# Feed-forward products in two passes: 512 columns over both halves of the activations, then 256

## The chip, the cores and the metric

The kernel runs on one core of a Trainium2 chip. The metric is the device time of one execution in microseconds (us): the kernel before takes 1524.75 us (median of three runs, 1522.54 to 1529.18). Lower is better.

## What is computed

Three layers over 256 tokens of 1024 features, in float32: two layers of a first block (feed-forward, mixer, feed-forward) and one of a second block (mixer, feed-forward). The change touches the five feed-forward stages alone:

```python
def swiglu(h, w_gate_up, w_down):          # four times, first block
    a, b = jnp.split(h @ w_gate_up, 2, axis=-1)
    return (jax.nn.silu(a) * b) @ w_down
x = x + 0.5 * swiglu(rms_norm(x, g), w_gate_up, w_down)

h2 = rmsnorm(x, norm2_w)                   # once, second block
a, v = jnp.split(h2 @ ffn_w_up, 2, axis=-1)
a = jax.nn.gelu(causal_dwconv(a, ffn_conv_w, ffn_conv_b), approximate=False)
x = x + (a * v) @ ffn_w_down               # 1024 -> 2 * 2816, then 2816 -> 1024
```

## The kernel before

**Products.** A float32 product is made of three: each operand is cut into a high and a low half (`wh`, `wl` of the weights, `ahi`, `alo` of the activations), and `mm3` (lines 192 to 194) adds `wl`·`ahi`, `wh`·`alo` and `wh`·`ahi` in one PSUM bank. Features stand on the partitions: a tile of 128 x 128 weights is the stationary operand, 256 tokens are the moving one. Below, a triple is the three products of one weight tile.

**Weights.** They stream from HBM in units of 128 x 2048 (1 MB, 16 weight tiles), in the order of use. `split` (line 151 is its VectorE half) cuts them, in feed-forward stages half a unit at a time: ScalarE copies 128 x 1024 (`wh<-raw`, line 86, the copy helper), VectorE subtracts (`wl<-raw,wh`). Three units lie raw, four are split (`SPLITS`): while a chunk of two units is in use, the two of the next are split.

**Order.** The program is written out by hand, in one order per engine. `tick()` stands after each step of products; it emits deferred work that is due (`defer(n, f)`: n ticks later), then one split. Each engine works its list strictly in order.

**A feed-forward stage.** `feed_forward` takes eleven chunks of 512 weight columns: four column tiles of 128, of which 0 and 2 are gates and 1 and 3 the ungated halves; each tile has eight k-tiles, so 32 triples a chunk. In `cols` a tick stands after every four triples. `emit` works on pairs: VectorE multiplies the gate by the norm's factor (`sl<-ps,rbc`, line 436), ScalarE takes Silu (line 437), VectorE multiplies by the other half (`hh<-ps,sl`, line 422), ScalarE cuts the high half (`ahi<-hh`), GpSimd subtracts for the low one (`alo<-hh,ahi`, line 421). In the second block the gate goes through a convolution (lines 443 to 450) and Gelu. Then `rows_out` makes the down projection, eight column tiles of 22 triples each; `add_to_x` adds each onto the residual stream `xT` with two VectorE instructions (lines 375, 376), and `Norm.done` cuts it for the next stage. The first stage has its first two chunks in `opening`, the others chunk 0 in `cols` with the norm's mean between.

Of the kernel before, what the change touches and what calls it, by code (L numbers as in the profile page):

```python
# [8 lines left out]
F = mybir.dt.float32  # L9
R = mybir.dt.float32r  # L10
# [4 lines left out]
P = 128  # L15
# [16 lines left out]
# columns of the row parameters  # L32
# [3 lines left out]
def weave(main, fill, ratio=1.0):  # L36
    """emit main's steps with `ratio` steps of fill after each"""
    due = 0.0
    for _ in main:
        due += ratio  # L40
        while due >= 1.0:
            next(fill, None)
            due -= 1.0


def drain(gen, plan={}):
    """emit gen to its end; plan[n] is emitted after its step n"""
    for n, _ in enumerate(gen):
        if n in plan:
            plan[n]()  # L50
# [3 lines left out]
def tile_hybrid_stack(ctx, tc, wts, cst, prm, rows, small, out, x):  # L54
# [4 lines left out]
    up = pool("acts", 35)  # L59
# [28 lines left out]
    class Acts:  # L88
        """activations split for the products, features on the partitions, one k-tile of 128 at a time"""

        def __init__(self):
            self.t = {}

        def get(self, k):
            if k // 2 not in self.t:
# [8 lines left out]
    # the weights' stream: (source, elements per partition) in the order of use  # L104
# [32 lines left out]
    def split(m):  # L137
        """m quarters of the next unit"""
# [18 lines left out]
    # work of the other engines that is emitted some steps of dense products later  # L157
# [12 lines left out]
    def tick():  # L170
        """what the other engines do beside a step of dense products"""
# [8 lines left out]
    def units(n, more=False):  # L180
        """the next n units; all before them are done with, but for `more` of the last ones"""
# [14 lines left out]
    def col_part(ps, acts, nk, unit_, k0, c0, pitch=512):  # L196
        """four k-tiles of a tile of 128 weight columns (on partitions) times all tokens"""
# [6 lines left out]
    def cols(acts, nk, emit, norm=None):  # L204
        """a chunk of 512 weight columns; emit(i, ps, ps) gets column tiles 2i and 2i + 1"""
# [26 lines left out]

    def opening(norm, emit0, emit1):
        """the first two chunks, k-tile by k-tile as they arrive; the mean of squares comes last"""
# [24 lines left out]
    def toks(acts, emit, n=512, norm=None):  # L259
        """all tokens (on partitions) times a chunk of n weight columns; emit(t, ps)"""  # L260
# [64 lines left out]
    class Norm:  # L325
        """the residual stream's tiles as they are done: split for the products, and their mean square"""

        def __init__(self, gcol):
            self.gcol = gcol
            self.acts = Acts()  # L330

        def done(self, j):
            """tile j of the residual stream is final"""
# [35 lines left out]
    def add_to_x(norm, scale, rb):  # L369
        def emit(j, ps):  # L370
            if rb is None:
                nc.vector.tensor_tensor(xT[:, j], ps, xT[:, j], OP.add)
            else:
                d = wt("dx")
                nc.vector.tensor_tensor(d, ps, rb, OP.mult)  # L375
                nc.vector.scalar_tensor_tensor(xT[:, j], d, scale, xT[:, j], op0=OP.mult, op1=OP.add)  # L376
            if norm is None:
                nc.sync.dma_start(out[:, j], xT[:, j])
            else:
                norm.done(j)  # L380
        return emit

# [23 lines left out]
    def feed_forward(norm, gate, nxt, scale, first=False, beside=None):  # L406
        """up and gate projections with features on the partitions; the norm's factor of the
        ungated half is applied to the sums of the down projection, which it commutes with"""
        hT = Acts()
        pace[0] = 2  # L410

        def emit(j):
            def f(i, pg, pu, both=None):
                k = 2 * j + i
                a, n = gate(k, pg)
                v = wt("hh")

                def last():
                    dh, dl = hT.get(k)
                    copy(dh, v)  # L420
                    nc.gpsimd.tensor_tensor(dl, v, dh.bitcast(F), OP.subtract)  # L421
                defer(n, lambda: nc.vector.tensor_tensor(v, pu, a, OP.mult))  # L422
                defer(n + 1, last)
            return f
# [9 lines left out]
    def silu_gate(f, ps):  # L434
        a = wt("sl")
        nc.vector.tensor_tensor(a, ps, RS["bc"], OP.mult)  # L436
        nc.scalar.activation(a, a, AF.Silu)  # L437
        return a, 1

    def conv_gate(f, ps):  # L440
        w = lambda k: pr[:, P_FCW + 3 * f + k:P_FCW + 3 * f + k + 1]
        z, a = wt("cz"), wt("sl")
        nc.vector.tensor_tensor(z, ps, RS["bc"], OP.mult)
        nc.scalar.activation(a, z, AF.Identity, scale=w(2), bias=pr[:, P_FCB + f:P_FCB + f + 1])
# [4 lines left out]
        defer(1, rest)  # L449
        defer(2, lambda: nc.scalar.activation(a, a, AF.Gelu))  # L450
        return a, 3

# [1 line left out]
    def rope_tables(col, rcol, n, name):  # L454
        """the gains folded into the rotation's tables, for n gains of 64"""
# [24 lines left out]
    def head_roots(sq, n, d, name):  # L480
        """(mean of squares + eps) ** -0.5 of sq [P, n, d] -> [P, n]"""
# [16 lines left out]
    def to_heads(src, dst, t):  # L498
        """[P, 512] -> dst [2] x [P, 2, S], features on the partitions"""
# [70 lines left out]
    def soft_rows(ps, mask, nscale, mn, rsum, p):  # L570
        """s = (ps + mask) * nscale, mn = min of s; p = exp(mn - s), rsum = its row sums"""
# [9 lines left out]
    def staged(n, *stages):  # L581
        """software pipeline: in round r, stage (lag, f) of item r - lag"""
# [7 lines left out]
    def mixer1(l, norm, nxt, tables):  # L590
# [51 lines left out]
        def window_means(k, t):  # L642
            """mean of the last 2 ** (k + 1) tokens less the token itself"""
# [106 lines left out]
    def mixer2(norm, nxt, tables):  # L750
# [13 lines left out]
        # mLSTM queries (k-tiles 0, 1) and keys (2, 3): causal convolution along the tokens  # L764
# [22 lines left out]
        # kw | vw | small gates  # L787
# [9 lines left out]
        # log forget gates, both token tiles at once: log_sigmoid(f) = min(f, 0) - log1p(exp(-|f|)),  # L797
        # log1p(e) = 2 atanh(e / (2 + e))
# [45 lines left out]
        # mLSTM heads  # L844
# [93 lines left out]
        # attention queries  # L938
# [49 lines left out]
        def windows(i):  # L988
            """the blocks to compress: [(half, d), l, (group, n)], half h holding position l + 16 h"""
# [54 lines left out]
        # attention over the selected (0) and window (1) branches  # L1044
# [45 lines left out]
        # the compressed branch  # L1090
# [112 lines left out]
    norm = Norm(P_L)  # L1203
# [7 lines left out]
    for l in range(2):  # L1211
# [6 lines left out]
        norm, nxt = nxt, Norm(pb + 16)  # L1218
        mixer1(l, norm, nxt, tabs)
        norm, nxt = nxt, Norm(P_L + P_LN if l == 0 else P_N1)  # L1220
# [4 lines left out]
    nxt = Norm(P_N2)  # L1225
# [35 lines left out]
def _rows_of(w, kt):  # L1261
    """[K, N] -> units of kt k-tiles, each [128, kt, N] in memory order"""
# [4 lines left out]
def _tiles_of(w):  # L1267
    """[K, N] -> units of 16 tiles [128, 128], column tile by column tile"""
# [94 lines left out]
```

## Time and profile before

| | |
|---|---|
| time, median of 3 runs | 1524.75 us (1522.54 to 1529.18) |
| profiled execution, first to last instruction (its span; its own time is not given) | 1519.0 us |
| granted TensorE clock, mean | 0.998 |
| busy: TensorE, VectorE, ScalarE, GpSimd | 99%, 65%, 50%, 21% |
| DMA | 261.86 MB, mean 172 GB/s |

In the rows PE is TensorE's matmuls, PEld its weight loads, DVE VectorE, ACT ScalarE, POOL GpSimd. A matmul's duration overlaps that of its neighbours, so what one costs is the distance between two starts. A row of the timeline gives start and length in us; "x2" is two instructions merged; brackets hold the idle time before and who ended it.

### The profile page before, as it was taken

The page shows a single profiled execution, that of the slowest core. Times are in us where ns is not written, and L with a number is a line of the kernel's source. Part 1 is how long each engine was busy: PE and PEld are TensorE (multiplying, and loading weights), DVE is VectorE, ACT ScalarE, POOL GpSimd, SP SyncE. Part 2 cuts the span into 40 slices and gives each one's busy share as a digit, 9 for nine tenths or more (in the row PEclk, how much of TensorE's full clock was granted, in tenths as well). Part 3 has the DMA queues.
Part 4 walks back from the last instruction along what each step waited for, and adds up shares of the span by engine and source line. Part 5 has one row for each costly group of instructions (what it writes and reads, how often), then busy time and mean ns, then how long its engine had stood idle before and what let it go on. Part 6 is the DMA issues. An engine that isn't in the chain of part 4 may idle for free. (4 is left out here: it accounts for less than half of the span.)

```text
span 1519.0 us, 28268 instructions
## 1 busy us (share of the span) xinstructions
PE 1500.6 (99%) x11806; PEld 1455.6 (96%) x11806; DVE 981.6 (65%) x1503; ACT 752.2 (50%) x1275; POOL 321.8 (21%) x393
## 2 busy tenths in 40 slices
PE   7999999999999999999999999999999999999998
PEld 7999988999999999999989999999987889999998
DVE  6666568577655655656585686566676667877662
ACT  5544345455444444444455654444457736555541
POOL 3311144013111121111360042111233011421200
PEclk9999999999999999999999999999999999999999
DMA  7555535444555544555443455556443423555551
GB/s 283 187 185 201 198 122 191 140 159 175 183 181 192 205 157 172 190 194 194 175 167 112 167 170 191 190 172 214 162 167 111 167 84 138 184 181 192 194 213 39
DMA packets 38720, 261.86 MB, mean 172 GB/s; under 512 B 4288, under 2 KB 5824, under 8 KB 7744
## 3 DMA queue, kind: packets, MB, share of 16 engines
q1 hardware_dynamic: 38016, 259.08, 48.2%
q8 instruction: 92, 1.51, 0.4%
q10 hardware_dynamic: 576, 0.98, 0.2%
q14 instruction: 36, 0.29, 0.1%
HBM read 258.99 MB, written 1.05 MB: 171 GB/s over the span
## 5 line engine op out<-in xcount | busy, mean ns | idle before, releaser
L192 PE MATMUL ps<-ahi,wl 128*128 128x256 f32 x3472 | 994.7, 286 | 8.0 <-DVE wl L151 7.1
L193 PE MATMUL ps<-alo,wh 128*128 128x256 f32 x3472 | 983.6, 283 | 0.0
L194 PE MATMUL ps<-ahi,wh 128*128 128x256 f32 x3472 | 983.4, 283 | 0.0
L151 DVE TENSOR_TENSOR wl<-raw,wh 128x1024 fp32r<-128x1024 f32 (+2 forms) x605 | 639.6, 1095 | 116.7 <-ACT wh L86 116.1
L192 PEld LDWEIGHTS ps<-ahi,wl 128*128 128x128 f32 x3472 | 667.1, 192 | 19.4 <-DVE wl L151 9.9
L193 PEld LDWEIGHTS ps<-alo,wh 128*128 128x128 f32 x3472 | 667.5, 192 | 0.3
L194 PEld LDWEIGHTS ps<-ahi,wh 128*128 128x128 f32 x3472 | 667.2, 192 | 0.0
L86 ACT ACTIVATE wh<-raw 128x1024 fp32r<-128x1024 f32 (+2 forms) x605 | 506.7, 881 | 69.0 <-PE ps L194 33.1
L421 POOL TENSOR_TENSOR alo<-hh,ahi 128x256 fp32r<-128x256 f32 x110 | 98.3, 894 | 493.0 <-ACT ahi L86 492.8
L437 ACT ACTIVATE sl<-sl 128x256 f32<-128x256 f32 x88 | 36.6, 417 | 218.1 <-DVE sl L436 218.0
L86 ACT ACTIVATE ahi<-xT,pr 128x256 fp32r<-128x256 f32 x64 | 32.2, 507 | 154.9 <-DVE xT L376 119.5
L422 DVE TENSOR_TENSOR hh<-ps,sl 128x256 f32<-128x256 f32 x108 | 45.6, 423 | 64.2 <-ACT sl L437 54.0
L436 DVE TENSOR_TENSOR sl<-ps,rbc 128x256 f32<-128x256 f32 x86 | 36.4, 424 | 78.0 <-PE ps L194 75.7
L342 POOL TENSOR_TENSOR sq<-xT 128x256 f32<-128x256 f32 x56 | 36.8, 657 | 202.6 <-DVE xT L376 181.1
L375 DVE TENSOR_TENSOR dx<-ps,rbc 128x256 f32<-128x256 f32 x40 | 17.0, 425 | 88.2 <-PE ps L194 88.2
L192 PE MATMUL ps<-wh,alo 128*128 128x512 f32 (+1 forms) x176 | 69.9, 397 | 0.0
L193 PE MATMUL ps<-wl,ahi 128*128 128x512 f32 (+1 forms) x176 | 67.8, 385 | 1.3 <-DVE wl L151 1.3
L86 ACT ACTIVATE ahi<-hh 128x256 fp32r<-128x256 f32 x110 | 44.9, 410 | 46.8 <-DVE hh L422 46.8
L194 PE MATMUL ps<-wh,ahi 128*128 128x512 f32 (+1 forms) x176 | 67.8, 385 | 0.0
L346 DVE SCALAR_TENSOR_TENSOR alo<-xT,pr,ahi 128x256 fp32r<-128x256 f32 x64 | 36.2, 569 | 30.0 <-ACT ahi L86 29.9
L560 POOL TENSOR_TENSOR alo<-g,ahi 128x512 fp32r<-128x512 f32 x9 | 13.3, 1483 | 182.0 <-ACT ahi L86 182.0
L343 POOL TENSOR_TENSOR sums<-sums,sq 128x256 f32<-128x256 f32 x56 | 49.2, 878 | 4.4
(251 smaller groups left out, 963.5 us busy)
## 6 DMA issues: line engine op xcount, KB each, us to landing
raw<-wts SPq DMA_DIRECT2D x241, 1024.0 KB, 4.8
raw<-wts SPq DMA_DIRECT2D x2, 576.0 KB, 4.3
raw<-wts SPq DMA_DIRECT2D x4, 256.0 KB, 5.7
raw<-wts SPq DMA_DIRECT2D x2, 512.0 KB, 8.2
out_dram<-xT SPq DMA_DIRECT2D x8, 128.0 KB, 1.9
cs<-cst SPq DMA_DIRECT2D x1, 565.0 KB, 7.2
xT<-x SPq DMA_DIRECT2D x1, 512.0 KB, 7.2
pw<-pool_w ACTq DMA_DIRECT2D x2, 256.0 KB, 3.4
```

Source lines behind the costliest of these rows:

```text
L86: nc.scalar.activation(dst, src, AF.Copy, **kw)
L151: nc.vector.tensor_tensor(lo[:, c], raw[:, c], hi[:, c].bitcast(F), OP.subtract)
L192: nc.tensor.matmul(ps, ll, rh, start=start, stop=False)
L193: nc.tensor.matmul(ps, lh, rl, start=False, stop=False)
L194: nc.tensor.matmul(ps, lh, rh, start=False, stop=stop)
L342: nc.gpsimd.tensor_tensor(sq, xT[:, j], xT[:, j], OP.mult)
L343: nc.gpsimd.tensor_tensor(self.sums, self.sums, sq, OP.add)
L346: nc.vector.scalar_tensor_tensor(dl, xT[:, j], gain, dh.bitcast(F), op0=OP.mult, op1=OP.subtract)
L421: nc.gpsimd.tensor_tensor(dl, v, dh.bitcast(F), OP.subtract)
L422: defer(n, lambda: nc.vector.tensor_tensor(v, pu, a, OP.mult))
L436: nc.vector.tensor_tensor(a, ps, RS["bc"], OP.mult)
L437: nc.scalar.activation(a, a, AF.Silu)
```

## The change

In the feed-forward stages the two halves of an activation tile now lie side by side in one tile (`ahl`, 128 x 512: high, then low). For each column tile `passes` makes eight matmuls of 512 columns (`wh` against both halves), a tick, then eight of 256 (`wl` against the high halves) into the bank's first half. A bank so holds `wh`·hi + `wl`·hi in its first 256 columns and `wh`·lo in its second, and the two have to be added:

- up projection (`wide_cols`, `halves`): ScalarE copies the second half out of PSUM (`wb<-ps`), VectorE adds it to the first (`sl<-ps,wb` or `hh<-ps,wb`), GpSimd multiplies the gate by the norm's factor (`sl<-sl,rbc`) and later the two halves of the pair (`hh<-hh,sl`), both VectorE's before; ScalarE's cut and GpSimd's subtraction stay.
- down projection (`wide_rows`, `add_halves`): ScalarE copies the second half, scaled; GpSimd multiplies it by the norm's factor and adds it onto `xT`; VectorE does the first half as before, one tick later. Each tile is worked in groups of 8, 8 and 6 k-tiles.
- left as before: chunk 0 (the first two chunks in the first stage), the last column tile of each down projection, and both mixers, which keep `mm3`. `acts`, the buffers of activations, goes from 35 to 33; three buffers `wb` of 128 x 256 are new.

TensorE has 2,338 triples of two matmuls in place of three: 1,568 in up projections, 770 in down projections.

```diff
-    up = pool("acts", 35)
+    up = pool("acts", 33)
...
+    def passes(ps, tiles, acts, nk):
+        for k, wh, _ in tiles:
+            nc.tensor.matmul(ps, wh, acts.both(k), start=k == 0, stop=False)
+        tick()
+        yield
+        for k, _, wl in tiles:
+            nc.tensor.matmul(ps[:, 0], wl, acts.both(k)[:, 0], start=False, stop=k == nk - 1)
+
+    def wide_cols(acts, emit):
+        us = units(2)
+        for i in range(4):
+            ps = mm_bank()
+            tiles = [(k, *(u[:, k % 4 * 512 + i * P:k % 4 * 512 + (i + 1) * P] for u in us[k // 4])) for k in range(KT)]
+            yield from passes(ps, tiles, acts, KT)
+            emit(i, ps)
+            tick()
+            yield
...
+    def second_half(ps, **kw):
+        t = sp.tile([P, S], F, tag="wb", name="wb", bufs=3)
+        copy(t, ps[:, 1], **kw)
+        return t
+
+    def add_halves(norm, scale, rb):
+        def emit(j, ps):
+            t, d = second_half(ps, scale=scale), wt("dx")
+            nc.gpsimd.tensor_tensor(t, t, rb, OP.mult)
+            nc.gpsimd.tensor_tensor(xT[:, j], xT[:, j], t, OP.add)
+            nc.vector.tensor_tensor(d, ps[:, 0], rb, OP.mult)
+            defer(1, lambda: onto_x(j, d, norm, scale))
+        return emit
...
+        def halves(j):
+            gated = []
+            def f(i, ps):
+                k = 2 * j + i // 2
+                t = second_half(ps)
+                def add():
+                    z = wt("hh" if i % 2 else "sl")
+                    nc.vector.tensor_tensor(z, ps[:, 0], t, OP.add)
+                    if i % 2 == 0:
+                        nc.gpsimd.tensor_tensor(z, z, rb(), OP.mult)
+                        gated.append(gate(k, z, 1))
+                        return
+                    a, n = gated.pop()
+                    n = max(n - 2, 1)
+                    defer(n, lambda: nc.gpsimd.tensor_tensor(z, z, a, OP.mult))
+                    defer(n + 1, lambda: cut(k, z))
+                defer(1, add)
+            return f
...
-        for j in range(2 if first else 0, 11):
-            drain(cols(norm.acts, KT, emit(j), None if j else norm))
+        if not first:
+            drain(cols(norm.acts, KT, emit(0), norm))
+        for j in range(2 if first else 1, 11):
+            drain(wide_cols(norm.acts, halves(j)))
         flush()
-        drain(rows_out(hT, FT, add_to_x(nxt, scale, RS["bc"])))
+        drain(wide_rows(hT, FT, add_halves(nxt, scale, rb()), add_to_x(nxt, scale, rb())))
```

What this does to the lists of the engines is seen at two places of the first up projection. On ScalarE one chunk stood so (`sl` is Silu, `ahi` the cut of the product):

```order
L86 ACTIVATE wh_740<-raw_536 128x1024 x2
L86 ACTIVATE wh_769<-raw_627 128x1024
L437 ACTIVATE sl_787<-sl_787 128x256
L86 ACTIVATE wh_769<-raw_627 128x1024
L86 ACTIVATE ahi_807<-hh_790 128x256
L437 ACTIVATE sl_850<-sl_850 128x256
L86 ACTIVATE ahi_807<-hh_853 128x256
```

and one chunk stands so in the changed kernel (`wb` is the copy of a bank's second half):

```order
L552 ACTIVATE sl_825<-sl_825 128x256
L86 ACTIVATE wh_840<-raw_732 128x1024
L86 ACTIVATE wb_854<-ps_830 128x256
L86 ACTIVATE wh_840<-raw_732 128x1024
L86 ACTIVATE wb_881<-ps_860 128x256
L86 ACTIVATE ahl_883<-hh_856 128x256
L552 ACTIVATE sl_886<-sl_886 128x256
L86 ACTIVATE wb_907<-ps_889 128x256
L86 ACTIVATE wh_921<-raw_759 128x1024
L86 ACTIVATE wb_932<-ps_911 128x256
L86 ACTIVATE ahl_934<-hh_909 128x256
L86 ACTIVATE wh_921<-raw_759 128x1024
```

Four copies are new, and the weight splits stand singly between a Silu, copies and cuts. On VectorE one chunk and the start of the next stood so:

```order
L436 TENSOR_TENSOR sl_787<-ps_725,rbc_393 128x256
L422 TENSOR_TENSOR hh_790<-ps_725,sl_787 128x256
L151 TENSOR_TENSOR wl_770<-raw_627,wh_769 128x1024 x2
L436 TENSOR_TENSOR sl_850<-ps_794,rbc_393 128x256
L422 TENSOR_TENSOR hh_853<-ps_794,sl_850 128x256
L151 TENSOR_TENSOR wl_871<-raw_666,wh_870 128x1024 x2
```

and stand so now (`sl<-ps,wb` is the addition of a gate's halves, `hh<-ps,wb` that of the other column tile):

```order
L160 TENSOR_TENSOR wl_1146<-raw_983,wh_1145 128x1024 x2
L523 TENSOR_TENSOR hh_1192<-ps_1166,wb_1190 128x256
L160 TENSOR_TENSOR wl_1177<-raw_1068,wh_1176 128x1024 x2
L523 TENSOR_TENSOR sl_1222<-ps_1196,wb_1217 128x256
L523 TENSOR_TENSOR hh_1245<-ps_1225,wb_1243 128x256
L523 TENSOR_TENSOR sl_1273<-ps_1247,wb_1268 128x256
```

Each addition of a tile now stands alone behind its own copy, and a pair's second addition follows two subtractions of weights. GpSimd's list, which had the subtraction `alo<-hh,ahi` alone, is for each pair: `sl<-sl,rbc`, `hh<-hh,sl`, `ahl<-hh,ahl` (lines 525, 530 and 511 of the changed kernel). No DMA is added, and SyncE's list is the same.

## Rows read from the trace of the kernel before

**Rows 1.** The page, part 1: span; busy time, share of it and instructions by engine.

```profile
span 1519.0 us, 28268 instructions
...
PE 1500.6 (99%) x11806; PEld 1455.6 (96%) x11806; DVE 981.6 (65%) x1503; ACT 752.2 (50%) x1275; POOL 321.8 (21%) x393
```

**Rows 2.** The table of stretches: a feed-forward stage, busy us and (instructions) by engine.

```profile
40.00:198.00 158.00, 158.00 (x1319) 158.00 (x1319) 98.25 (x117) 74.69 (x105) 31.80 (x47) 1.00 0.53 187
```

**Rows 3.** Who waited for whom on TensorE: us in total, times, longest us.

```profile
PE ps L192 <- DVE wl L151: 7.1, 7, 5.8
```

**Rows 4.** Timeline of TensorE, up projection: start, us; first and last of 28.

```profile
599.74 0.28 PE L194 MATMUL ps<-ahi,wh 128*128 128x256 f32 x1
...
602.98 0.28 PE L194 MATMUL ps<-ahi,wh 128*128 128x256 f32 x1
```

**Rows 5.** Timeline of TensorE, mixer projection with 512 columns: first and last of 20.

```profile
203.61 0.39 PE L194 MATMUL ps<-wh,ahi 128*128 128x512 f32 x1
...
207.93 0.39 PE L192 MATMUL ps<-wh,alo 128*128 128x512 f32 x1
```

**Rows 6.** Groups of VectorE, shapes apart: busy us, mean ns; idle before, releaser.

```profile
L422 DVE TENSOR_TENSOR hh<-ps,sl 128x256 f32<-128x256 f32 x108 | 45.6, 423 | 64.2 <-ACT sl L437 54.0 <-ACT sl L450 8.8 <-PE ps L194 1.3
...
L447 DVE SCALAR_TENSOR_TENSOR sl<-cz,pr,sl 128x255 f32<-128x255 f32 x22 | 10.7, 487 | 14.2 <-ACT sl L444 14.1
```

**Rows 7.** Groups of ScalarE, shapes apart: a copy out of PSUM of 256 columns.

```profile
L86 ACT ACTIVATE rbc<-rb 128x256 f32<-128x256 f32 x8 | 3.1, 382 | 24.0 <-PE rb L364 24.0
```

**Rows 8.** Line 421, GpSimd: duration ns least/median/most, first and last start.

```profile
L421 POOL TENSOR_TENSOR alo<-hh,ahi x110: 735/745/1664, 39.8 to 1455.4; 128x256 fp32r<-128x256 f32 x110
```

**Rows 9.** Timeline of VectorE at three places where GpSimd works beside it.

```profile
66.14 0.42 DVE L422 TENSOR_TENSOR hh<-ps,sl 128x256 f32<-128x256 f32 x1 [0.61 <-ACT sl L437]
66.49 2.89 DVE L151 TENSOR_TENSOR wl<-raw,wh 128x1024 fp32r<-128x1024 f32 x2
...
223.79 2.13 DVE L151 TENSOR_TENSOR wl<-raw,wh 128x512 fp32r<-128x512 f32 x2
...
1341.50 2.36 DVE L151 TENSOR_TENSOR wl<-raw,wh 128x1024 fp32r<-128x1024 f32 x2 [0.53 <-ACT wh L86]
```

**Rows 10.** Timeline of GpSimd at the same three places.

```profile
67.38 0.92 POOL L421 TENSOR_TENSOR alo<-hh,ahi 128x256 fp32r<-128x256 f32 x1 [5.29 <-ACT ahi L86]
...
224.16 1.22 POOL L477 TENSOR_TENSOR sq<-qk 128x512 f32<-128x512 f32 x1 [1.08 <-ACT qk L86]
225.34 1.18 POOL L471 TENSOR_TENSOR rb<-qk,tks 128x256 f32<-128x256 f32 x1
...
1342.80 1.66 POOL L421 TENSOR_TENSOR alo<-hh,ahi 128x256 fp32r<-128x256 f32 x1 [3.07 <-ACT ahi L86]
```

**Rows 11.** Timeline of ScalarE in an up projection.

```profile
65.62 0.42 ACT L437 ACTIVATE sl<-sl 128x256 f32<-128x256 f32 x1 [1.52 <-DVE sl L436]
65.95 1.04 ACT L86 ACTIVATE wh<-raw 128x1024 fp32r<-128x1024 f32 x1
...
72.68 2.94 ACT L86 ACTIVATE wh<-raw 128x1024 fp32r<-128x1024 f32 x3
```

**Rows 12.** Timeline of TensorE around two waits of the second mixer.

```profile
1126.76 0.50 PE L193 MATMUL ps<-wl,ahi 128*128 128x512 f32 x1 [1.33 <-DVE wl L151]
1127.10 0.40 PE L194 MATMUL ps<-wh,ahi 128*128 128x512 f32 x1
...
1151.19 0.92 PE L1055 MATMUL at<-KT,qT 64*128 64x128 f32 x4 [2.86 <-DVE mn L572]
...
1152.63 0.63 PE L193 MATMUL ps<-wl,ahi 128*128 128x512 f32 x1
1153.06 0.63 PE L194 MATMUL ps<-wh,ahi 128*128 128x512 f32 x1
```

More of the change, by code (lines that the diff above doesn't have):

```diff
@@ L88, in tile_hybrid_stack, with __init__, both @@
     class Acts:
-        def __init__(self):
-            self.t = {}
+        def __init__(self, wide=False):
+            self.t, self.wide = {}, wide
+        def both(self, k):
+            if k not in self.t:
+                self.t[k] = ut([P, 2, S], "ahl", R)
+            return self.t[k]
         def get(self, k):
+            if self.wide:
+                t = self.both(k)
+                return t[:, 0], t[:, 1]
             if k // 2 not in self.t:
@@ L231, in cols, with wide_rows, tile @@
                     yield
+    def passes(ps, tiles, acts, nk):
[14 more added lines that the diff above has]
+            yield
+    def wide_rows(acts, nk, emit, narrow):
+        u0, us = n_used[0], {}
+        def tile(n):
+            return tuple(u[:, n % 16 * P:(n % 16 + 1) * P] for u in us[n // 16])
+        for j in range(KT):
+            ps = mm_bank()
+            for k0 in range(0, nk, 8):
+                ks = range(k0, min(k0 + 8, nk))
+                first, final = j * nk + ks[0], j * nk + ks[-1]
+                n_held[0] = u0 + first // 16
+                for m in range(first // 16, final // 16 + 1):
+                    if m not in us:
+                        us[m] = units(1, True)[0]
+                tiles = [(k, *tile(j * nk + k)) for k in ks]
+                if j < KT - 1:
+                    yield from passes(ps, tiles, acts, nk)
+                    if ks[-1] == nk - 1:
+                        emit(j, ps)
+                else:
+                    for n, (k, wh, wl) in enumerate(tiles):
+                        mm3(ps[:, 0], wh, wl, *acts.get(k), k == 0, k == nk - 1)
+                        if n == 3:
+                            tick()
+                            yield
+                    if ks[-1] == nk - 1:
+                        narrow(j, ps[:, 0])
+                tick()
+                yield
     def opening(norm, emit0, emit1):
@@ L325, in tile_hybrid_stack, with __init__ @@
     class Norm:
-        def __init__(self, gcol):
+        def __init__(self, gcol, wide=False):
             self.gcol = gcol
-            self.acts = Acts()
+            self.acts = Acts(wide)
         def done(self, j):
@@ L375, in emit, with onto_x @@
                 nc.vector.tensor_tensor(d, ps, rb, OP.mult)
[L376 to L380, printed above, removed]
+                onto_x(j, d, norm, scale)
+                return
+            norm.done(j)
+        return emit
+    def onto_x(j, d, norm, scale):
+        nc.vector.scalar_tensor_tensor(xT[:, j], d, scale, xT[:, j], op0=OP.mult, op1=OP.add)
+        if norm is None:
+            nc.sync.dma_start(out[:, j], xT[:, j])
+        else:
+            norm.done(j)
+    def second_half(ps, **kw):
[9 more added lines that the diff above has]
+            defer(1, lambda: onto_x(j, d, norm, scale))
         return emit
@@ L406, in feed_forward @@
     def feed_forward(norm, gate, nxt, scale, first=False, beside=None):
-        hT = Acts()
+        hT = Acts(True)
         pace[0] = 2
+        rb = lambda: RS["bc"]
         def emit(j):
@@ L448, in rest @@
             nc.vector.scalar_tensor_tensor(a[:, 2:], z[:, :S - 2], w(0), a[:, 2:], op0=OP.mult, op1=OP.add)
-        defer(1, rest)
-        defer(2, lambda: nc.scalar.activation(a, a, AF.Gelu))
-        return a, 3
+        defer(1 + later, rest)
+        defer(2 + later, lambda: nc.scalar.activation(a, a, AF.Gelu))
+        return a, 3 + later
     def rope_tables(col, rcol, n, name):
@@ L1200, in mixer2 @@
         drain(rows_out(mT, KT, add_to_x(nxt, 1.0, None)))
-    norm = Norm(P_L)
+    norm = Norm(P_L, True)
     for j in range(KT):
```

42 lines of the change are left out of this document (24 added, 18 removed).

## The prediction

> **What bounds the kernel now.** Read first the page's busy times: VectorE is busy for 982 of 1519 us, ScalarE for 752, GpSimd for 322 [rows 1]. TensorE is the bound: in the first feed-forward stage it is busy for all of 158.00 us at a granted clock of 1.00 [rows 2], and in the whole span its largest wait on one producer is 7.1 us in seven pieces, all but 1.3 of it one piece of 5.8 [rows 3]. So a feed-forward stage lasts as long as its matmuls. What one costs is the distance of starts, not its 0.28 us: 28 matmuls of 256 columns start 0.120 us apart (602.98 - 599.74, over 27) [rows 4]; 20 of 512 columns start 0.227 us apart (207.93 - 203.61, over 19) [rows 5]. The difference, 0.107 us, is 256 columns at 2.4 GHz; so each matmul has a fixed 0.0133 us beside its columns.
>
> **What is saved.** A triple costs 3 x 0.120 = 0.360 us; now 0.227 + 0.120 = 0.3467. All its columns are still there; one fixed part is gone. Over 2,338 triples that is 31.2 us: 20.9 in up projections, 10.3 in down projections. A chunk of 32 triples goes from 11.52 to 11.09 us. DMA then has to bring its two units (2 MB) in 11.09 us, 189 GB/s; it does 187 in that stage now [rows 2]. I cost that at nothing.
>
> The Trainium skill (TensorE: Matmul & The Clock Gate, Back-to-back issue gap) gives an isolated matmul a fixed part of about 2.5 ns; by that the saving would be an estimated 2,338 x 2.5 ns = 6 us. The rows show 13.3 ns here, and I go by them.
>
> **What is added, by sums.** Per chunk ScalarE gets four PSUM copies of 0.38 us [rows 7], and GpSimd six instructions in place of two, each 0.74 us when alone [rows 8]; VectorE has as many as before (four of 0.42, [rows 9]). ScalarE then has four splits that hold it 0.95 each ((2.94 - 1.04)/2) and eight small ones at 0.33 (65.62 to 65.95) [rows 11], 6.4 of 11.09 us. VectorE has four subtractions of weights and four additions, 4 x 1.14 + 4 x 0.34 = 5.9; GpSimd 4.4. By sums all fit. In the old stage they also fitted, with GpSimd at 31.8 of 158 us [rows 2].
>
> **What is added, by the chain.** Each list is worked in order, and the lists now hand to each other at every tile. Two things make this long.
>
> First, VectorE's subtraction of weights and a GpSimd instruction don't run together. At 1341.50 two subtractions end at 1343.86 (1.22 us each, starts 1.14 apart) and the GpSimd one issued at 1342.80 ends 0.60 after them, having taken 1.66 instead of 0.74 [rows 9, 10]. At 67.38 GpSimd got in between two subtractions: it ended at 68.30, and the second subtraction 1.08 later, so that the pair took 2.89 instead of 2.36. They take turns in order of arrival: at 224.16 VectorE came second and still went ahead of GpSimd's next instruction, which was queued already and took 1.18.
>
> Second, the additions (one operand in PSUM) are not held up, but each waits for a copy on ScalarE, and that stands behind a Silu that waits for GpSimd.
>
> Once the chain is behind TensorE, one turn of a chunk is, from Silu to Silu: ScalarE Silu 0.33, copy 0.33, split 0.95, copy 0.38; handover 0.10 (66.14 less the Silu's end at 66.04, [rows 9, 11]); VectorE add 0.34, subtraction 1.22; GpSimd's subtraction 0.60 after it; VectorE's second 1.08; GpSimd's multiplication by the norm's factor 0.60; handover at most 0.10: 6.0. Then Silu 0.33, split 0.95, copy 0.38, handover 0.10, add 0.34, subtraction 1.22, GpSimd's product 0.60, subtraction 1.08, GpSimd's subtraction 0.60, its multiplication 0.74, handover at most 0.10: 6.4. In all 12.4 us; with handovers from GpSimd near nothing, 12.2. I take 12.35 against TensorE's 11.09: **each chunk the weights come 1.26 us later.**
>
> How much lag is free: the chunk's last low part is ready 11.0 us after its Silu (all above but the last 1.4). TensorE asks for it in the second pass of the next chunk's first tile, 11.09 + 8 x 0.227 + 6 x 0.120 = 13.6 us after the chunk's start: 2.6 us. In the first wide chunk the first addition can't start before TensorE has done the tile, at 2.8; from there the chain has 10.3 us left, less about 1.2 since GpSimd's subtraction of the pair before comes early enough to take no turn: it ends at about 11.9, 0.6 to 0.8 late. By the start of the ninth of ten wide chunks the lag is 0.6 + 7 x 1.26 = 9.4, of which 2.6 is free: TensorE waits 6.8 us in an up projection. The down projection asks for the last product about 6.7 us after its start, and the lagging chain (then some 5 us behind, with 3.4 us still to do for it) has it at 8.4: 1.7. Each wait also costs the matmul behind it: after a wait of 1.33 us the next start came 0.34 later, not 0.23 [rows 12]; six of these are 0.6. Sum 9.1 us a stage: three stages 27.3; the first with nine wide chunks 7.8; the last, where the convolution's two instructions of 0.49 [rows 6] stand in the chain beside a longer tail, 10.5. In three stages twelve small GpSimd instructions for rotation tables stand in its list; 1 us each. Together 48.6 us.
>
> **Costed at nothing.** In a down projection GpSimd's two new instructions lengthen the way from a tile to its split by about 2 us out of 7.6; two units split ahead (11 us) cover it; without that cover it is 2 us a tile, 70 us. The last column tile is as before, so the hand-over to the next stage is too. The smaller buffer pool adds waits in the mixers; bounds 0 (the buffers are long free) and 3 us (the largest wait there now is 2.86, [rows 12]); I take 0, as most are on instructions off TensorE's path. The clock: after 2.86 us idle, matmuls of 512 columns started 0.43 apart (1152.63 to 1153.06), 1.2 GHz, after 1.33 us they did not fall [rows 12]; the waits here are of 1.3, so nothing, but it stands close.
>
> **Sum.** -31.2 + 48.6 = +17.4 on a span of 1519.0: 1536. The median of the runs, 1524.75, lies 5.75 above the span, which holds what lies around it; the time is then 1542, and I say 1541.
>
> **Rivals.**
>
> - *The chain keeps pace (faster).* All turns on one point: whether GpSimd's subtraction for the pair before comes before or after the chunk's first subtraction of weights. In the lagging chain I find it 0.17 us after. Coming before, it costs no turn, Silu starts 1.1 us earlier, the turn of a chunk is 11.2 us, and lag stays within the free 2.6 us. Then only the saving is left, 1493.5, and with a few waits up to 1500. For it: the margin is less than two handovers. Against it: once behind, nothing brings the chain back until the down projection.
> - *Half way.* A turn of 11.7 us gives 0.6 a chunk: 0.6 + 7 x 0.6 - 2.6 = 2.2 of waits, with 2 for the end and the rest some 5 a stage, 25 in all: 1519, no change.
> - *Whole turns (slower still).* If whoever loses waits for the whole 0.74 us and then needs its whole 1.22, the chain has 0.14 more at each of four GpSimd places and 0.28 in all more at the two subtractions behind them: 13.2 us, 2.1 a chunk, 15 us a stage: 1570. The Trainium skill (SBUF — State Buffer, Who interferes with whom) states it so: whoever issues first has the shared pair for the whole instruction, and the other fully blocks. The trace agrees that one blocks (1.66 for 0.74), but the handover came earlier than that [rows 9, 10].
> - *The change does not save what it says:* were the fixed part not per matmul, the waits alone would remain, 1573. Rows 4 and 5 speak against it.
>
> **How the numbers follow.** My forecast has 0.47, of which 0.04 falls inside half a per cent (about 7.6 us, what a measurement of this kernel can tell from no change); keeping pace 0.33; half way 0.13; whole turns and no saving 0.07 together. So faster 0.33, same 0.17, slower 0.50. The forecast's own range is 1527 to 1560 (a turn 0.3 us shorter or longer moves five stages by some 17 us). Leaving out keeping pace would leave out 3 in 10, so the range starts at its middle: 1495 to 1562.
>
> **What would show it.** Right: in up projections TensorE waits on VectorE's `wl`, about 1.3 us once a chunk from the fourth or fifth wide chunk on, chunks 12.3 us apart there and 11.1 at the stage's start; matmuls 0.227 and 0.120 apart; GpSimd's instructions between two subtractions of weights longer than 0.74; down projections without waits after their first tile, 7.63 us a tile. Wrong: chunks at 11.1 us throughout, or GpSimd's subtraction ahead of the chunk's first `wl`; a wait on copies or PSUM banks in place of `wl`; a granted clock below 1.00 in a feed-forward stage.

## The result, and the profile after

The changed kernel takes 1544.58 us (median of four runs, 1539.78 to 1548.28); the kernel before, run beside it, 1526.64 (1522.54 to 1529.18). The ratio is 1.0134, with a 95% interval of [1.0104, 1.0164]: 1.3% slower. The forecast was 1541. The span grew by 20.2 us, from 1519.0 [rows 1] to 1539.2; the forecast had 17.4. The profiled execution itself took 1541.0.

The page of the changed kernel, part 1:

```profile
span 1539.2 us, 24143 instructions
...
PE 1486.2 (97%) x9468; PEld 1333.1 (87%) x9468; DVE 1008.2 (66%) x1503; ACT 818.3 (53%) x1506; POOL 665.7 (43%) x659
```

Against [rows 1], TensorE has 2,338 matmuls fewer and falls from 99% to 97%; VectorE has the same 1503 instructions; ScalarE has 231 more and GpSimd 266 more, and GpSimd's busy time doubles. Only TensorE comes near the whole span, so by shares alone no other engine would be in its way. Who waited for whom on TensorE (us in total, times, longest us) says more:

```profile
PE ps L251 <- DVE wl L160: 26.1, 34, 1.0
PE ps L201 <- DVE wl L160: 8.7, 9, 7.1
PE ps L247 <- POOL ahl L511: 6.8, 5, 2.1
...
PE ps L247 <- ACT wh L86: 0.5, 1, 0.5
```

The second row is nearly all the opening, which is in [rows 3] too; its one long wait is 1.3 us longer in this execution (7.1 in place of 5.8). The other three are new: 34 waits of the 256-column pass (line 251) for a low part of weights, one wait at the start of each of the five down projections, for the last activations, and a single short one for a high half of weights. On the timeline of TensorE the waits stand like this in the second feed-forward stage, and at the start of the last down projection (start, length, in brackets the idle time and who ended it):

```profile
381.92 2.00 PE L247 MATMUL ps<-ahl,wh 128*128 128x512 f32 x8
...
426.61 2.00 PE L247 MATMUL ps<-ahl,wh 128*128 128x512 f32 x8
428.45 0.87 PE L251 MATMUL ps<-ahl,wl 128*128 128x256 f32 x6
429.77 0.50 PE L251 MATMUL ps<-ahl,wl 128*128 128x256 f32 x2 [0.45 <-DVE wl L160]
...
466.31 0.51 PE L251 MATMUL ps<-ahl,wl 128*128 128x256 f32 x2 [0.75 <-DVE wl L160]
466.65 2.01 PE L247 MATMUL ps<-ahl,wh 128*128 128x512 f32 x8
...
478.49 0.50 PE L251 MATMUL ps<-ahl,wl 128*128 128x256 f32 x2 [0.74 <-DVE wl L160]
478.83 2.00 PE L247 MATMUL ps<-ahl,wh 128*128 128x512 f32 x8
...
507.47 0.51 PE L247 MATMUL ps<-ahl,wh 128*128 128x512 f32 x1 [1.17 <-POOL ahl L511]
...
531.59 2.00 PE L247 MATMUL ps<-ahl,wh 128*128 128x512 f32 x8
...
539.27 2.00 PE L247 MATMUL ps<-ahl,wh 128*128 128x512 f32 x8
...
1478.49 0.50 PE L247 MATMUL ps<-ahl,wh 128*128 128x512 f32 x1 [2.14 <-POOL ahl L511]
...
1479.55 3.29 PE L247 MATMUL ps<-ahl,wh 128*128 128x512 f32 x8
```

The first wide chunk starts at 381.92, the fifth at 426.61: 11.17 us each, no wait. From the fifth to the tenth there is one wait a chunk, always before the last two of eight matmuls of the first tile's low pass, where the last half of the chunk's second unit is asked for. These six waits stand 12.18 us apart (478.49 - 466.31). So a chunk that needs 11.17 us of TensorE takes 12.18.

The groups of GpSimd's and ScalarE's instructions (busy us, mean ns | idle before, releaser):

```profile
L511 POOL TENSOR_TENSOR ahl<-hh,ahl 128x256 fp32r<-128x256 f32 x110 | 138.2, 1257 | 67.7 <-ACT ahl L86 67.7
L530 POOL TENSOR_TENSOR hh<-hh,sl 128x256 f32<-128x256 f32 x78 | 93.4, 1197 | 139.1 <-DVE hh L523 135.1
...
L525 POOL TENSOR_TENSOR sl<-sl,rbc 128x256 f32<-128x256 f32 x98 | 119.4, 1219 | 29.8 <-DVE sl L523 29.8
L552 ACT ACTIVATE sl<-sl 128x256 f32<-128x256 f32 x88 | 36.7, 418 | 169.6 <-POOL sl L525 168.2
```

Each kind of GpSimd's three instructions per pair takes 1.2 us on the mean, where one alone takes 0.74 [rows 8]. And ScalarE has sat for 168.2 us in front of its 88 Silus, waiting for GpSimd's multiplication; behind each stand a copy or a weight split that needed nothing of it. That number alone proves nothing. In the kernel before, ScalarE sat even longer in front of the same 88 Silus, waiting for VectorE, and TensorE hardly waited [rows 3]:

```profile
L437 ACT ACTIVATE sl<-sl 128x256 f32<-128x256 f32 x88 | 36.6, 417 | 218.1 <-DVE sl L436 218.0
```

Whether the wait matters is for the experiments.

### The profile page after: what moved, and what is told of

The parts are those of the page before. It is cut to its first block, busy times and chain, and to the rows that moved or that the text cites. A ratio compares the mean times of both kernels' runs of the same rounds, so it can differ in the third digit from the quotient of the medians.

```text
span 1539.2 us, 24143 instructions
## 1 busy us (share of the span) xinstructions
PE 1486.2 (97%) x9468; PEld 1333.1 (87%) x9468; DVE 1008.2 (66%) x1503; ACT 818.3 (53%) x1506; POOL 665.7 (43%) x659
## 5 line engine op out<-in xcount | busy, mean ns | idle before, releaser
L247 PE MATMUL ps<-ahl,wh 128*128 128x512 f32 x2338 | 590.0, 393 | 8.0 <-POOL ahl L511 6.8
L247 PEld LDWEIGHTS ps<-ahl,wh 128*128 128x128 f32 x2338 | 420.2, 189 | 85.4 <-POOL ahl L511 9.0
L251 PEld LDWEIGHTS ps<-ahl,wl 128*128 128x128 f32 x2338 | 322.5, 190 | 56.5 <-DVE wl L160 33.0
L251 PE MATMUL ps<-ahl,wl 128*128 128x256 f32 x2338 | 336.5, 284 | 26.1 <-DVE wl L160 26.1
L201 PE MATMUL ps<-ahi,wl 128*128 128x256 f32 x864 | 253.1, 293 | 0.4 <-DVE wl L160 0.4
L202 PE MATMUL ps<-alo,wh 128*128 128x256 f32 x864 | 244.0, 282 | 0.0
L203 PE MATMUL ps<-ahi,wh 128*128 128x256 f32 x864 | 244.0, 282 | 0.0
L201 PEld LDWEIGHTS ps<-ahi,wl 128*128 128x128 f32 x864 | 165.0, 191 | 10.5 <-issue 7.6
L202 PEld LDWEIGHTS ps<-alo,wh 128*128 128x128 f32 x864 | 165.2, 191 | 0.2
L203 PEld LDWEIGHTS ps<-ahi,wh 128*128 128x128 f32 x864 | 165.0, 191 | 0.0
L525 POOL TENSOR_TENSOR sl<-sl,rbc 128x256 f32<-128x256 f32 x98 | 119.4, 1219 | 29.8 <-DVE sl L523 29.8
L552 ACT ACTIVATE sl<-sl 128x256 f32<-128x256 f32 x88 | 36.7, 418 | 169.6 <-POOL sl L525 168.2
L201 PE MATMUL ps<-ahl,wl 128*128 128x256 f32 x270 | 79.3, 294 | 8.4 <-DVE wl L160 8.3
```

What stands on the lines that cost most here:

```text
L201: nc.tensor.matmul(ps, ll, rh, start=start, stop=False)
L202: nc.tensor.matmul(ps, lh, rl, start=False, stop=False)
L203: nc.tensor.matmul(ps, lh, rh, start=False, stop=stop)
L247: nc.tensor.matmul(ps, wh, acts.both(k), start=k == 0, stop=False)
L251: nc.tensor.matmul(ps[:, 0], wl, acts.both(k)[:, 0], start=False, stop=k == nk - 1)
L525: nc.gpsimd.tensor_tensor(z, z, rb(), OP.mult)
```

## The experiments

The theory is the prediction's: in an up projection the lists of ScalarE, VectorE and GpSimd form a chain. It goes round once per chunk in 12.2 us, through ScalarE's waiting Silu and through the turns that VectorE and GpSimd take; whoever makes the chain shorter takes the waits away. There are two rivals. One is the load: VectorE and GpSimd hold each other up, and there is too much work of both, in whatever order (below, the load theory). The other is the units' way from memory. All kernels are the changed one with the edit shown. For each stage, time is counted from its matmul that spreads the norm's factor (`rb<-dg,ones`) to the next one of the kind, and in the last stage to TensorE's end.

**The Silu one step later in the lists, and the same kernel a second time.** The instructions are the same, only their order differs. In the last stage it is the whole gate, the convolution and Gelu, that comes a step later.

```diff
-                        gated.append(gate(k, z, 1))
+                        gated.append(gate(k, z, 2))
```

> One number is changed: the gate's Silu stands one tick later in ScalarE's list, behind the next tile's copy and split instead of ahead of them, so that these no longer wait for GpSimd. Nothing is added or removed. If the chain through all three lists sets the pace (12.2 us a chunk against TensorE's 11.1), cutting it here leaves some 9.8 us a chunk: TensorE's waits on wl in the up projections (34 of them, 26 us) go, those at the start of the down projections (6.8 us) shrink, and the time is 1505 to 1512 us, 2 to 2.5% below the changed kernel and 1% below the kernel before. If VectorE and GpSimd together have too much work that needs their shared reading, or if the weights come too late from memory, the same work is still there: waits and time stay, 1540 to 1548.

> The same kernel as silu_late, on the same chip as both_late for the comparison: 1501 to 1507 us, no waits on wl in the up projections; the span differs from the first time's only by how long the half clock lasts in the second mixer (13.6 us of half clock there).

Measured: 1503.45 us, ratio to the kernel before 0.9863 [0.9837, 0.9889]; the second time 1501.46, 0.9866 [0.9848, 0.9884]. It beats both kernels, and the first time lies below its range of 1505 to 1512. TensorE's waits, the group of Silus, a chunk on ScalarE's timeline and TensorE's passes, all of the first of the two:

```profile
PE ps L201 <- DVE wl L160: 8.1, 6, 7.0
PE at L1170 <- DVE mn L687: 2.9, 1, 2.9
PE ps L247 <- POOL ahl L511: 2.4, 1, 2.4
```

```profile
L552 ACT ACTIVATE sl<-sl 128x256 f32<-128x256 f32 x88 | 36.6, 417 | 11.7 <-POOL sl L525 9.2 <-DVE sl L501 1.4
```

```profile
106.69 2.00 ACT L86 ACTIVATE wh<-raw 128x1024 fp32r<-128x1024 f32 x2
108.89 0.38 ACT L86 ACTIVATE wb<-ps 128x256 f32<-128x256 f32 x1 [0.21 <-PE ps L251]
109.31 0.42 ACT L552 ACTIVATE sl<-sl 128x256 f32<-128x256 f32 x1
109.64 1.05 ACT L86 ACTIVATE wh<-raw 128x1024 fp32r<-128x1024 f32 x1
```

```profile
425.81 2.00 PE L247 MATMUL ps<-ahl,wh 128*128 128x512 f32 x8
427.65 1.12 PE L251 MATMUL ps<-ahl,wl 128*128 128x256 f32 x8
428.60 2.00 PE L247 MATMUL ps<-ahl,wh 128*128 128x512 f32 x8
```

All 34 waits on `wl` are gone, and ScalarE's wait for GpSimd is 9.2 us in place of 168.2: two splits and a copy are now done while GpSimd multiplies. GpSimd's multiplications by the norm's factor are as long as they were (1218 ns on the mean, 1219 in the changed kernel), so the two engines still hold each other up, and TensorE no longer waits for it. Work, operands and loads from memory are the same, so neither the load by itself nor the units' way was the cause. A tile of eight k-tiles takes 2.79 us here (428.60 - 425.81), a chunk 11.17.

**The cut one step later.** This takes GpSimd's subtraction out from between the addition and the multiplication.

```diff
-                    defer(n + 1, lambda: cut(k, z))
+                    defer(n + 2, lambda: cut(k, z))
```

> The cut of the pair before (ScalarE's copy, GpSimd's subtraction) is put one tick later, so that GpSimd's multiplication of the gate comes ahead of that subtraction. If it is this subtraction's turn between VectorE's first two subtractions of weights that makes the chain too long, one turn of each (0.60 + 1.08 us) leaves the way to the Silu, a chunk needs 10.5 us, and TensorE's waits on wl go: 1507 to 1515 us, with the waits at the start of the down projection left (the last product is cut later). If load or memory is the cause: 1540 to 1548 as before.

Measured: 1507.16 us, 0.991 [0.9877, 0.9942]. Waits on `wl` fell from 26.1 us in 34 to 5.6 in 9, all in the first and the last stage; the three stages between take 185.9, 186.8 and 185.9 us, to 0.1 us what they take with the Silu moved. The waits at the start of the down projections, expected to stay, are gone but for 1.7 us in the last. So the prediction's turning point, whether GpSimd's subtraction stands ahead of its multiplication in the lagging chain, is one of the links; ScalarE's order is another, and either is enough in these stages.

**Both later.**

> The chain theory: with the Silu one step later the up projections of the four Silu stages have no waits on wl left, so putting the cut one step later as well has nothing to take away there; the one wait left is 2.4 us at the start of the last down projection, and a later cut can only lengthen it. Stages in the middle 185.5 to 187, time 1500 to 1508, the same as with the Silu alone to within 0.3%. If some other resource (the copies, the pool of buffers, the weights' loads) still held the stages back, two steps of more room would show: under 1497.

Measured: 1501.93 us, 0.9846 [0.9814, 0.9878]: by the medians the same as the Silu alone (1501.46, 0.9866 on the same chip). In the profile, though, the wait of 2.4 us at the last down projection, which I thought could only grow, is gone too, and the last stage takes 177.0 us in place of 181.2. The span did not show it, since the second block's mixer, where nothing differs, took 236.9 us in this execution, at a mean granted clock of 0.95, and 228.0 in the other, at 0.99. Of the executions with a mean clock of 0.999 the one here took 1493.41 us and the one with the Silu alone 1499.91, so the 4 us are there. No new wait comes to light under the old ones.

**The multiplication on VectorE.**

```diff
-                        nc.gpsimd.tensor_tensor(z, z, rb(), OP.mult)
+                        nc.vector.tensor_tensor(z, z, rb(), OP.mult)
```

> The multiplication of the gate by the norm's factor goes back from GpSimd to VectorE (98 instructions of some 0.43 us there, 98 of 0.74 here fewer). By the chain, Silu then follows two VectorE instructions and waits for no turn: about 9.7 us a chunk, no waits on wl, 1503 to 1512 us. By load, VectorE has 0.85 us a chunk more and the shared reading is asked for about as much as before: the waits shrink by a third at most, 1530 to 1545.

Measured: 1507.48 us, 0.9894 [0.9868, 0.992]. VectorE, the busier of the two engines, has 98 instructions more, and the kernel is faster than both; 5.6 us of waits on `wl` are left, all in the last stage. The chain has a handover less, but this run alone does not part the theories: GpSimd's busy time falls too, from 665.7 to 518.9 us, while VectorE's grows from 1008.2 to 1039.9. By the load theory the time was to stay at 1530 or more.

**One GpSimd instruction more, ahead of the gate's multiplication or behind it.** It multiplies the norm's factor by itself into a tile that nobody reads; the two kernels differ in one line's place. The lines that allocate the tile are the same in both and not shown.

Ahead:

```diff
+                        nc.gpsimd.tensor_tensor(junk[0], rb(), rb(), OP.mult)
                         nc.gpsimd.tensor_tensor(z, z, rb(), OP.mult)
```

Behind:

```diff
                         nc.gpsimd.tensor_tensor(z, z, rb(), OP.mult)
+                        nc.gpsimd.tensor_tensor(junk[0], rb(), rb(), OP.mult)
```

> GpSimd gets one idle multiplication more per pair (0.74 us, into a buffer that nobody reads), ahead of the gate's multiplication in its list. By the chain it lies on the way to the Silu in both pairs of a chunk: a chunk's turn grows by 1.4 us to 13.6, some nine chunks in five stages, and the time is 1590 to 1610 us. By load alone (GpSimd goes from 4.4 to 5.9 of 11.1 us a chunk) this run and the one with the same instruction put behind would be alike.

> The same idle GpSimd multiplication per pair as in the run before, but behind the gate's multiplication in GpSimd's list, where GpSimd waits for VectorE's next addition anyway (from 5.9 to 8.2 us of a chunk's turn). By the chain it costs nothing: 1540 to 1550 us, as the changed kernel. By load it costs what it cost in the other place: 1585 to 1595.

Measured, in two executions each: ahead 1590.35 us, 1.0432 [1.038, 1.0483]; behind 1550.8 us, 1.0181 [1.0131, 1.0231]. Two successive waits of the second stage, TensorE's timeline, ahead and then behind:

```profile
443.43 0.50 PE L251 MATMUL ps<-ahl,wl 128*128 128x256 f32 x2 [0.94 <-DVE wl L160]
...
456.75 0.50 PE L251 MATMUL ps<-ahl,wl 128*128 128x256 f32 x2 [0.94 <-DVE wl L160]
```

```profile
453.01 0.51 PE L251 MATMUL ps<-ahl,wl 128*128 128x256 f32 x2 [0.74 <-DVE wl L160]
465.18 0.50 PE L251 MATMUL ps<-ahl,wl 128*128 128x256 f32 x2 [0.74 <-DVE wl L160]
...
1395.62 0.50 PE L251 MATMUL ps<-ahl,wl 128*128 128x256 f32 x2 [1.17 <-DVE wl L160]
1408.60 0.51 PE L251 MATMUL ps<-ahl,wl 128*128 128x256 f32 x2 [1.17 <-DVE wl L160]
```

Ahead, a chunk is 13.32 us long (13.6 expected); behind, 12.17, as in the changed kernel. The load is the same 98 instructions. In the four Silu stages the one behind is free to 0.2 us (187.4, 193.1, 193.9, 193.2 against 187.2, 193.1, 194.0, 193.2), the one ahead costs 10 to 12 us in each. The load theory expected the two to be alike. My bound for gp_after, 1550, was passed by a little: in the last stage, with the convolution gate, it is on the chain (12.98 us a chunk, last two rows, against 12.37; the stage is 6.3 us longer), while the one ahead adds 0.2 us there. Which link of that gate is behind this I did not follow.

**Up projections alone, down projections alone.**

Up alone:

```diff
-            drain(wide_rows(hT, FT, add_halves(nxt, scale, rb()), add_to_x(nxt, scale, rb())))
+            drain(rows_out(hT, FT, add_to_x(nxt, scale, rb())))
```

Down alone:

```diff
-            drain(wide_cols(norm.acts, halves(j)))
+            drain(cols(norm.acts, KT, emit(j)))
```

> The up projections in two passes, the down projections as in the kernel before: 770 triples give back 0.0101 us each (0.3597 before, 0.3496 measured after), 7.8 us, and the last product is asked for some 0.8 us later in five stages. The waits on wl in the up projections stay as they are, since the chain there is the same. 1543 to 1553 us. If the down projection's new GpSimd work were part of the loss, the time would fall below the changed kernel's 1544.

> The down projections in two passes, the up projections as in the kernel before: 770 triples save 7.8 us, no chain that spans a chunk, no waits: 1514 to 1518 us. If GpSimd's two instructions on the way to a tile's split were not covered by the two units split ahead, the down projections would wait and the time would stay above 1520.

Measured: up alone 1544.03 us, 1.014 [1.0112, 1.0169]; down alone 1517.65 us, 0.9967 [0.9946, 0.9987], with TensorE waiting only where it does in the kernel before. So the waits that make the loss arise in the up projections. The down projections are 1.6 us faster in each stage by themselves; behind wide up projections they are worth 0.5 to 0.8 in the first four stages (187.2, 193.1, 194.0 and 193.2 us against 187.7, 193.7, 194.8 and 193.8 with up alone), and cost 0.6 in the last. Most of the rest goes into the wait at their start for activations that the lagging chain has not cut yet. With up alone TensorE's waits on `wl` and on that are:

```profile
PE ps L251 <- DVE wl L160: 26.0, 34, 1.0
...
PE ps L202 <- POOL ahl L511: 1.4, 5, 0.4
```

The wait at the start is 1.4 us, where the changed kernel has 6.8.

**The passes woven together,** on top of the Silu one step later: after each 512-column matmul of a k-tile its 256-column one, in place of eight and eight.

```diff
-        for k, wh, _ in tiles:
+        for n, (k, wh, wl) in enumerate(tiles):
             nc.tensor.matmul(ps, wh, acts.both(k), start=k == 0, stop=False)
-        tick()
-        yield
-        for k, _, wl in tiles:
             nc.tensor.matmul(ps[:, 0], wl, acts.both(k)[:, 0], start=False, stop=k == nk - 1)
+            if n == 3:
+                tick()
+                yield
```

> As the run with the late Silu, but the two matmuls of a triple follow each other (512 columns, 256 columns, next k-tile) in place of eight and eight. In passes the first five of eight 512-column matmuls stood 0.233, 0.236, 0.228, 0.232 and 0.231 us apart, the other three 0.2267. If each change from 256 to 512 columns costs this, 2,338 changes in place of 300 cost up to 15 us: 1503 to 1518. If it belongs to a run of matmuls of one kind (something that fills up over the first five), the 0.0265 us a pass goes and the time is 1494 to 1500. wl is asked for 1.6 us earlier in a chunk, which the chain without the Silu in it has to spare.

Measured: 1511.37 us, 0.9909 [0.988, 0.9939]; TensorE's timeline, first and last of 23 pairs:

```profile
431.93 0.40 PE L247 MATMUL ps<-ahl,wh 128*128 128x512 f32 x1
432.16 0.28 PE L248 MATMUL ps<-ahl,wl 128*128 128x256 f32 x1
...
439.69 0.40 PE L247 MATMUL ps<-ahl,wh 128*128 128x512 f32 x1
```

A pair takes 0.353 us ((439.69 - 431.93)/22), against 2.79/8 = 0.349 in blocks; each of the three middle stages is 1.9 us longer. By the distances of [rows 4, 5] it would be 0.227 + 0.120 = 0.347 in both. So what a matmul costs depends on its neighbours: eight k-tiles cost 0.02 us over that sum with one change from 512 to 256 columns, and 0.05 with eight. More changes cost more, as the first of the two expected cases had it, though not eight times as much.

## Why the prediction was right, and where its terms were off

Stages in us; "waits" is the changed kernel less the one with both steps later, "saved" that one less the kernel before:

| stage | before | after | both later | waits: forecast | measured | saved: measured |
|---|---|---|---|---|---|---|
| first | 181.4 | 187.2 | 177.0 | 8.8 | 10.1 | 4.4 |
| second | 191.0 | 193.1 | 185.9 | 9.1 | 7.2 | 5.1 |
| third | 191.9 | 194.0 | 186.8 | 10.1 | 7.2 | 5.1 |
| fourth | 191.0 | 193.2 | 185.9 | 10.1 | 7.3 | 5.1 |
| last | 182.1 | 190.2 | 177.0 | 10.5 | 13.2 | 5.1 |
| sum | 937.5 | 957.7 | 912.8 | 48.6 | 44.9 | 24.8 |

The five stages give -24.8 + 44.9 = +20.1 of the +20.2 us. What lies between them is equal but for 1.4 us more before the first stage and 1.3 less in the second block's mixer. The mechanism came as forecast; the closeness of the sum is in part luck, since the saving was forecast 6.4 us too large and the waits 3.7 too large, and the one error hides most of the other. The prediction also took the 5.75 us from span to median for what lies around the span. In the changed kernel only 1.8 us do (1541.0 - 1539.2); the rest of its 5.4 is that the profiled execution was faster than the median.

**What is saved** was forecast at 31.2 us and is 24.8. The term took 0.227 us for every 512-column matmul, from a row of twenty of them [rows 5]. In a pass of eight the start of the next pass comes after 1.84 us (427.65 - 425.81), not 8 x 0.227 = 1.81; a chunk is 11.17 us, not 11.09. Over 49 chunks that is 3.9 us; a tile of a down projection takes 7.68 us (539.27 - 531.59) and not 7.63, 1.8 us over 35. That is 5.7 of the 6.4 missing. The Trainium skill (TensorE: Matmul & The Clock Gate, Back-to-back issue gap) gives an isolated matmul a fixed part of about 2.5 ns, by which the saving would be an estimated 6 us; the measured 24.8 is against it here. The Trainium skill says there that this is the gap of a matmul by itself, and that in a stream of weight loads and matmuls the spacing differs from it.

**The chain** was forecast at 12.2 to 12.4 us a turn and takes 12.18 in the Silu stages. Its links stand on the timelines of VectorE, GpSimd and ScalarE in the changed kernel's first stage:

```profile
105.23 0.42 DVE L523 TENSOR_TENSOR sl<-ps,wb 128x256 f32<-128x256 f32 x1 [0.79 <-ACT wb L86]
105.57 2.89 DVE L160 TENSOR_TENSOR wl<-raw,wh 128x1024 fp32r<-128x1024 f32 x2
110.84 0.42 DVE L523 TENSOR_TENSOR hh<-ps,wb 128x256 f32<-128x256 f32 x1 [2.38 <-ACT wb L86]
```

```profile
105.79 1.59 POOL L511 TENSOR_TENSOR ahl<-hh,ahl 128x256 fp32r<-128x256 f32 x1 [0.53 <-ACT ahl L86]
107.35 1.72 POOL L525 TENSOR_TENSOR sl<-sl,rbc 128x256 f32<-128x256 f32 x1
```

```profile
109.10 0.42 ACT L552 ACTIVATE sl<-sl 128x256 f32<-128x256 f32 x1 [2.44 <-POOL sl L525]
109.43 1.04 ACT L86 ACTIVATE wh<-raw 128x1024 fp32r<-128x1024 f32 x1
110.37 0.37 ACT L86 ACTIVATE wb<-ps 128x256 f32<-128x256 f32 x1
```

The first subtraction of weights starts at 105.57; GpSimd's subtraction comes at 105.79, 0.22 us later, where 0.17 was forecast, and so takes a turn. It ends at 107.38; the multiplication, whose operand had been ready since 105.65, runs after the second subtraction, from 107.35 to 109.07, 0.61 behind VectorE's end at 108.46 (forecast 0.60). Only then can the Silu start, at 109.10, and only behind it the next split and copy, for which VectorE sits idle for 2.38 us. The order that hangs on this margin of 0.22 us, and on which the rival "the chain keeps pace" turned, decided the sign: with the cut one step later the chain does keep pace but in the first and last stage, at 1507 us, and with the Silu later in all, at 1501 to 1503, where that rival had 1493.5 to 1500. The additions were not held up, as said: the 76 of 196 that ran beside a GpSimd instruction took 417 ns on the mean, the others 422.

**The waits.** Forecast: one a chunk from the fourth or fifth wide chunk on, 1.26 us of new lag each. Found in the second stage: from the fifth on, 1.01 us each (12.18 - 11.17; the slower matmuls leave less to wait for), and 1.2 at the down projection's start, where 1.7 was forecast. In the first stage the first wait comes in the second wide chunk already, and every later chunk has one; I had given this stage only one chunk less. On ScalarE's timeline the opening's last tiles hand over four Silus and four cuts between 38.8 and 43.6 us, when the wide chunks begin (37.5), which would leave the chain no head start; that this is the reason was not tested apart. In the last stage the wait at the down projection is 2.14 us long and is followed by a pass of 3.29 us in place of 2.00: the clock, which I had at 1.00 in feed-forward stages and called close, fell there, as one of the prediction's own signs of being wrong has it. The rotation tables cost their 1 us in the first stage alone. GpSimd's twelve instructions for them run there from 65.60 to 68.48 us, amid the wide chunks, and that turn is 13.19 us long (77.60 - 64.41), the next again 12.18; the single wait for a high half of weights (0.5 us, at 75.21) falls into it:

```profile
64.41 0.51 PE L251 MATMUL ps<-ahl,wl 128*128 128x256 f32 x2 [0.66 <-DVE wl L160]
...
77.60 0.50 PE L251 MATMUL ps<-ahl,wl 128*128 128x256 f32 x2 [0.95 <-DVE wl L160]
...
89.78 0.50 PE L251 MATMUL ps<-ahl,wl 128*128 128x256 f32 x2 [0.74 <-DVE wl L160]
```

The other two sets run about the start of the third and fourth stages (569.8 to 572.7 and 923.1 to 928.1), before the chain lags, and these stages have the second's 7.2 to 7.3 us of waits. So the middle stages came out below their forecast and the two ends above it, and the sum of the waits is near partly for that reason.

**The rivals.** "Whole turns" (13.2 us a turn) and "half way" (11.7) did not come: 12.18. The rule beside the first, from the Trainium skill (SBUF — State Buffer, Who interferes with whom), is that the port pair which VectorE and GpSimd share is an exclusive lock, and that the loser fully blocks. The Trainium skill says the second of VectorE instructions in a two-port mode; of those with two SBUF inputs, like the subtractions here, it says that they contend with a GpSimd instruction that reads SBUF. The trace agrees in that GpSimd's instructions took 1.59 and 1.72 us in place of 0.74, but each ended 0.6 us after VectorE's, not 0.74. "No saving" is refuted by the 24.8 us.

**Costed at nothing.** The down projections' two GpSimd instructions are hidden, as said: TensorE has no wait behind a down projection's first tile. The smaller pool of buffers cost nothing: the two first mixers take 158.1 and 158.2 us before and after. The clock cost about 1.6 us at the last down projection (3.29 - 2.00, and 1.44 in place of 1.11 for the pass of 256 columns behind it), not nothing; the 13.2 of the last stage holds it.

## What to carry to other kernels

When work of one engine is spread over three, don't stop at sums: write down each engine's list for one turn of the loop and follow it, with the durations that the instructions have when the engines work beside each other, and compare that turn with the time of the engine that bounds the kernel. If the turn is longer, try the order first: let the instruction that waits for another engine stand a step later, behind work that waits for nothing; here that one number turned 1.3% slower into 1.4% faster. And a price read from a long row of equal instructions need not hold where kinds change: here eight 512-column matmuls behind 256-column ones took 1.84 us and not 1.81.

## What the runs showed of the hardware

- After a wait of 2.14 us on TensorE the next full pass of eight 512-column matmuls took 3.29 us in place of 2.00, and the granted clock in that stretch was 0.82:

```profile
1478.00:1481.00 3.00, 2.51 (x12) 2.14 (x13) 2.39 (x3) 3.00 (x4) 0.44 (x1) 0.82 0.02 5
```

After the one of 1.17 us at 507.47 nothing fell. [Rows 12] had 1.33 without and 2.86 with a fall. But the length of the wait alone does not decide it. In the first run with the Silu one step later a wait of 2.35 us stands at the same place, and the next pass took 2.00 us at a granted clock of 1.00:

```profile
1444.85 0.49 PE L247 MATMUL ps<-ahl,wh 128*128 128x512 f32 x1 [2.35 <-POOL ahl L511]
...
1445.89 2.00 PE L247 MATMUL ps<-ahl,wh 128*128 128x512 f32 x8
```

With the GpSimd instruction added ahead, the waits at the first four down projections are 2.86 or 2.87 us; after two of them the clock fell to its lower level (0.60 on the mean over 529 to 533 us, 0.57 over 734 to 738), after the two others (166.08, 1097.60) it stayed at 1.00. One of 1.46 us in its first stage (77.37) was followed by a fall as well (0.53 over 79 to 82). So the prediction's step from [rows 12], that waits of 1.3 us do not make it fall, held in the changed kernel; which longer ones do, two waits could not tell.
- Eight 512-column matmuls after 256-column ones take 1.84 us from the first's start to the next pass, where eight of a long row of them take 1.81 [rows 5]; woven with 256-column ones, a pair costs 0.353 us in place of 0.349.
- One more GpSimd instruction per pair costs nothing (0.2 us at most) or 10 to 12 us in each of the four Silu stages, by its place in that engine's list alone. In the last stage the places change roles: 6.3 us behind, 0.2 ahead.
